# A hybrid decoder block on one core: the indexer's preparation taken off GpSimd, its key before the latents, the latents behind two more gate tiles

## The chip, the cores and the metric

One NeuronCore of a Trainium2 chip runs the whole kernel. The metric is device time in microseconds of one execution. Engines are named as in the profile: PE (TensorE matmul), PEld (its weight loads), DVE (VectorE), ACT (ScalarE), POOL (GpSimd) and SP (SyncE, which only issues transfers).

## The reference, cut to what matters

The block takes x (1024 tokens, 1024 channels), normalises it and projects it with one wide weight. The projection feeds a sparse attention whose 256 keys per query are picked by an indexer, a latent attention, and two sigmoid gates that merge them; a gated MLP with a causal convolution follows.

```python
hn = rmsnorm(h, norm_mix_g[l])
proj = jnp.einsum('bsd,de->bse', hn, w_in[l])
(a_q, a_k, a_v, i_q, i_k, i_w, b_cq, b_ckv, b_kr, g_a, g_b) = jnp.split(proj, IN_OFFSETS, axis=-1)
i_q = apply_rope(i_q.reshape(b, s, IDX_HEADS, IDX_DIM), cos_i, sin_i, IDX_ROT_DIM) * (IDX_DIM ** -0.5)
i_k = apply_rope(rmsnorm(i_k, idx_k_norm_g[l])[:, :, None, :], cos_i, sin_i, IDX_ROT_DIM)[:, :, 0, :]
o_a = indexed_sparse_attention(a_q, a_k, a_v, i_q, i_k, i_w, positions, topk)
c_q, c_kv = rmsnorm(b_cq, q_a_norm_g[l]), rmsnorm(b_ckv, kv_a_norm_g[l])
o_b = latent_attention(q_nope, q_rope, k_nope, k_rope, v_b, positions)
merged = jax.nn.sigmoid(g_a) * y_a + jax.nn.sigmoid(g_b) * y_b
```

Inside the sparse attention, for each block of 128 queries:

```python
dots = jnp.einsum('bqhd,bsd->bqhs', qib, ki)
iscore = jnp.einsum('bqh,bqhs->bqs', wib, jax.nn.relu(dots))
_, idx = lax.top_k(jnp.where(causal, iscore, -jnp.inf), topk)
```

## The kernel before, in words

**Products.** Every float32 operand is split into a high part (a copy into the fp32r type) and a low part (source minus high part). `mm3` (lines 176 to 189; the matmuls are L179, L180, L181) makes a product of three matmuls: high by high, high by low, low by high. `split` (L146) makes the parts: by default the high part is a copy on ACT (L149), the low part a subtraction on POOL (L155, which runs on DVE where a caller asks for it). `wload` (L521) fetches a piece of a weight through SP into one of three ring tiles (L496) and splits it.

**Stages around the change.** `load_x` loads and splits x and the weights `w_c2`. `chunk_kv` (L596) projects all eight blocks of 128 tokens with `w_c2` to 488 columns: the indexer's key (columns 0 to 63), its head weights (64 to 71), the query latent (72 to 327), the key latent (328 to 455) and the rotary key (456 to 487). ACT evacuates each block (L608) and takes sums of squares (L611). DVE then scales all three normalised parts (L627), applies the key's gain (L629), rotates the key and the rotary key (`rope`, L195 to L199), and SP stores the latents' rows to DRAM (L635, eight transfers). POOL writes the key twice, side by side (L638), so that a transpose on PE (L642) gives it on both halves of the partitions; ACT and DVE make its high and low parts (L643, L644).

`chunk_iq` (L671) projects the indexer's queries of blocks 2 to 7 with `w_c1`. `query` evacuates a block on ACT (L682) and rotates it on DVE; `stack` doubles its heads on POOL (`twice`, L660), transposes on PE (L651) and makes the parts on ACT and DVE (L653, L654). `indexer` (L729) then forms, head by head, scores on PE (L723), their relu on ACT (L742) and the weighted sum on DVE (L747). `chunk_a` (L966) projects the attention's queries and keys/values with `w_c3` and `w_c4` (four and two pieces of 128 x 1024) and stores them to DRAM through POOL's queue (L981). After that come the gate projections (`gates`, L985: eight weight tiles of `w_g` up to EARLY, then two up to NEXT; a tile is two halves of 512 tokens, each 24 matmuls; DVE takes each half out of PSUM, L1002). Beside them DVE searches the threshold of the top 256 (`guess`, L760; its counting step is L798).

`latents` (L1012) loads the stored rows again (L1021, six buffers), transposes them on PE (L1023) into three of the four single-bank PSUM tiles, and splits them (L1031, L1032). More gate tiles follow (10 to 13), then the latent attention. `prep_a` and `attn_a` (L1265, L1303) load the stored keys and queries for the sparse attention (L1274, L1297, L1314) and double them on POOL (L1275, L660) before the transposes.

**What sets the order.** The program text gives a priority; when the kernel is built, a planner simulates the engines and fixes one order of instructions for each engine. On the chip each engine and each issuing queue goes through its order and waits at the first instruction that is not ready. Tiles share memory: a tile whose place was used by an earlier one waits until that one is no longer read. The raw tiles of `chunk_iq` lie where `chunk_kv` kept its rows, so they also wait for the transfers of L635.

Of the kernel before, what the change touches and what calls it, by code (L numbers as in the profile page):

```python
# [10 lines left out]
F32 = mybir.dt.float32  # L11
# [6 lines left out]
OP = mybir.AluOpType  # L18
# [7 lines left out]
NKV = 2  # L26
# [82 lines left out]
class Block:  # L109
# [126 lines left out]
    def run(self):  # L236
# [55 lines left out]
        if self.causal:  # L292
            self.gates(None, go, range(EARLY, NEXT))
        self.latents(lat)
# [3 lines left out]
        self.gates(wg, go, range(NEXT if self.causal else 0, MID))  # L298
# [235 lines left out]
    def load_x(self, rawx, tmp):  # L534
# [9 lines left out]
        for kt in range(8):  # L544
            if kt == 2:
                self.prologue()
                if not self.causal:
                    self.positions(tmp)
            if kt == 0:
                w += self.cweights("w_c2", [0], "dve")  # L550
            st = self.t(rawx, [P, 1024], F32, tag="raw", bufs=3)
            parts = [slice(0, 512), slice(512, 1024)] if kt == 0 else [slice(0, 1024)]
            for cs in parts:
                nc.sync.dma_start(st[:, cs], a["xT"][kt * P:(kt + 1) * P, cs])
            if kt % 2 == 0 and kt:
                w += self.cweights("w_c2", [kt // 2], "dve")
# [24 lines left out]
    def cweights(self, name, js=range(4), eng_hi="act"):  # L581
        return [self.wload(self.w1, name, j, 4, eng_hi) for j in js]
# [13 lines left out]
    def chunk_kv(self, rawx, w):  # L596
# [22 lines left out]
        v.tensor_tensor(rs, rs, r3, op=OP.mult)  # L619
        self.iw = self.t(c, [P, NB, NH])  # L620
        v.tensor_scalar(self.iw, braw[:, :, HD:HD + NH], NH ** -0.5, None, op0=OP.mult)
        v.tensor_tensor(self.iw, self.iw, self.r[:, :, None].to_broadcast([P, NB, NH]), op=OP.mult)
        x = braw[:, :, 456:488]
        v.tensor_tensor(x, x, self.r[:, :, None].to_broadcast([P, NB, 32]), op=OP.mult)
        for k, (o, n) in enumerate(segs):
            x = braw[:, :, o:o + n]
            v.tensor_tensor(x, x, rs[:, k, :, None].to_broadcast([P, NB, n]), op=OP.mult)  # L627
        x = braw[:, :, :HD]
        v.tensor_tensor(x, x, self.gik[:, None, :].to_broadcast([P, NB, HD]), op=OP.mult)  # L629
        rt = self.kd[:, 768:].rearrange("p (b t n) -> p b t n", b=NB, t=2)  # L630
        self.rope(braw[:, :, 0:16].rearrange("p b (t n) -> p b t n", t=2), self.cos[:, :, ::2],
                  self.sin2[:, :, :, ::2], rt[:, :, :, 0:8])
        self.rope(braw[:, :, 456:488].rearrange("p b (t n) -> p b t n", t=2), self.cos, self.sin2, rt)
        for b in range(NB):
            nc.sync.dma_start(self.lat_d[b], braw[:, b, 72:W2N])  # L635
        kd = self.t(rawx, [P, S], F32, tag="raw", bufs=3)
# [7 lines left out]
        v.tensor_tensor(self.ikll, ps, self.ikhh.bitcast(F32), op=OP.subtract)  # L644

# [11 lines left out]
    def twice(self, pool, x, nh, tag, bufs=2):  # L657

        y = self.t(pool, [P, nh * 2 * HD], F32, tag=tag, bufs=bufs)
        self.nc.gpsimd.tensor_scalar(y.rearrange("p (h t d) -> p h t d", h=nh, t=2),  # L660
                                     x.rearrange("p (h d) -> p h d", h=nh)[:, :, None, :].to_broadcast([P, nh, 2, HD]),
                                     1.0, 0.0, op0=OP.mult, op1=OP.add)
        return y
# [7 lines left out]
    def chunk_iq(self, rp):  # L671
# [3 lines left out]
        w = self.cweights("w_c1")  # L675
# [11 lines left out]
        def stack(b):  # L687
            q[b] = self.qstack(self.twice(rp, raw[b], NH, "rawi", 1), IDX_SC, (8192, 5120, 4096)[b % 3])
# [576 lines left out]
    def prep_a(self):  # L1265
# [6 lines left out]
        def one(b):  # L1272
            raw = self.t(self.ring, [P, S], F32, tag="st", bufs=3)
            nc.sync.dma_start(raw[:, :256], self.akv_d[b])  # L1274
            nc.gpsimd.tensor_scalar(raw[:, 256:512].rearrange("p (h t d) -> p h t d", h=NKV, t=2),  # L1275
                                    raw[:, :P].rearrange("p (h d) -> p h d", h=NKV)[:, :, None, :]
                                    .to_broadcast([P, NKV, 2, HD]), 1.0, 0.0, op0=OP.mult, op1=OP.add)
# [17 lines left out]
        def first(n):  # L1295
            raw = self.t(self.ring, [P, S], F32, tag="st", bufs=3)[:, :512]
            nc.sync.dma_start(raw, self.aq_d[ORDER_A[n]])  # L1297
            self.qa.append(self.qstack(self.twice(self.ring, raw, NH, "st", 3), -SC_A, 7168 + 1024 * n))
# [4 lines left out]
    def attn_a(self, sp, ap, before, rest):  # L1303
# [738 lines left out]
```

## Time and profile before

| | us |
|---|---|
| three timed runs | 1594.61, 1597.29, 1597.31 |
| median | 1597.29 |
| the profiled execution, time | 1594.33 |
| the profiled execution, span of its instructions | 1592.5 |
| busy: PE, DVE, POOL, ACT | 1507.2, 1187.3, 910.5, 789.4 |

The span runs from the first to the last instruction; the time adds 1.8 us around it. A busy time is the union of the engine's instructions. "Idle before" an instruction is the gap on its own engine, put down to the work whose end released it.

### The profile page before, as it was taken

The page shows a single profiled execution, that of the slowest core. Times are in us where ns is not written, and L with a number is a line of the kernel's source. Part 1 is how long each engine was busy: PE and PEld are TensorE (multiplying, and loading weights), DVE is VectorE, ACT ScalarE, POOL GpSimd, SP SyncE. Part 2 cuts the span into 40 slices and gives each one's busy share as a digit, 9 for nine tenths or more (in the row PEclk, how much of TensorE's full clock was granted, in tenths as well). Part 3 has the DMA queues.
Part 4 walks back from the last instruction along what each step waited for, and adds up shares of the span by engine and source line. Part 5 has one row for each costly group of instructions (what it writes and reads, how often), then busy time and mean ns, then how long its engine had stood idle before and what let it go on. Part 6 is the DMA issues. An engine that isn't in the chain of part 4 may idle for free.

```text
span 1592.5 us, 21976 instructions
## 1 busy us (share of the span) xinstructions
PE 1507.2 (95%) x7586; PEld 1255.6 (79%) x7586; DVE 1187.3 (75%) x1860; ACT 789.4 (50%) x1454; POOL 910.5 (57%) x769
## 2 busy tenths in 40 slices
PE   9989999989899999999999989999999999989996
PEld 7768888867688877998878877888888887767874
DVE  7368999934588888885636668777777766896996
ACT  4545522223377788775434444444444444434445
POOL 4142122411667767654732399777777772487684
PEclk9989999999999999999999999999999999999999
DMA  7331133330300022213762132222222204964343
GB/s 256 108 105 46 54 105 97 111 115 27 106 14 17 14 83 93 76 56 118 238 198 87 53 93 80 80 80 82 81 84 84 85 36 162 329 210 127 126 137 123
DMA packets 74842, 166.25 MB, mean 104 GB/s; under 512 B 9634, under 2 KB 14114, under 8 KB 74722
## 3 DMA queue, kind: packets, MB, share of 16 engines
q1 hardware_dynamic: 62640, 139.59, 26.6%
q10 hardware_dynamic: 9490, 16.79, 2.8%
q0 software_dynamic: 2592, 8.39, 1.4%
q8 instruction: 61, 1.00, 0.3%
q14 instruction: 59, 0.48, 0.1%
HBM read 123.94 MB, written 40.53 MB: 103 GB/s over the span
## 4 chain that ended last, share of the span: by engine, by line
PE 66%; DVE 18%; issue 5%; ACT 4%; POOL 3%; DMA 3%; SPq 0%; ACTq 0%; DVEq 0%; POOLq 0%
PE tc L179 17%; PE tc L180 17%; PE tc L181 17%; PE tc L723 6%; DVE tc L155 3%; DVE tc L798 2%; DMA tc<-tc 2%; PE tc L1375 2%; PE tc L1228 2%; PE tc L1360 2%; PE tc L1209 1%; DVE tc L1136 1%; DVE tc L1002 1%; DVE tc L1159 1%; PE tc L651 1%
## 5 line engine op out<-in xcount | busy, mean ns | idle before, releaser
L179 PE MATMUL tc<-tc,tc 128*128 128x512 f32 (+2 forms) x1464 | 542.7, 374 | 9.7 <-ACT tc L1561 2.7
L181 PE MATMUL tc<-tc,tc 128*128 128x512 f32 (+2 forms) x1464 | 544.1, 372 | 4.3 <-DVE tc L155 4.3
L180 PE MATMUL tc<-tc,tc 128*128 128x512 f32 (+2 forms) x1464 | 544.3, 372 | 1.4 <-POOL tc L155 1.4
L155 POOL TENSOR_TENSOR tc<-tc,tc 128x512 fp32r<-128x512 f32 (+2 forms) x182 | 301.0, 1660 | 267.0 <-ACT tc L149 253.7
L149 ACT ACTIVATE tc<-tc 128x512 fp32r<-128x512 f32 (+1 forms) x362 | 230.5, 659 | 352.4 <-PE tc L180 242.1
L179 PEld LDWEIGHTS tc<-tc,tc 128*128 128x128 f32 x1464 | 277.3, 190 | 61.5 <-ACT tc L1561 3.0
L181 PEld LDWEIGHTS tc<-tc,tc 128*128 128x128 f32 x1464 | 277.3, 189 | 54.6 <-DVE tc L155 4.8
L180 PEld LDWEIGHTS tc<-tc,tc 128*128 128x128 f32 x1464 | 277.7, 190 | 50.5 <-POOL tc L155 2.1
L155 DVE TENSOR_TENSOR tc<-tc,tc 128x512 fp32r<-128x512 f32 x184 | 224.4, 1253 | 46.2 <-ACT tc L149 46.0
L180 PE MATMUL tc<-tc 128*128 128x512 f32 (+1 forms) x380 | 149.4, 395 | 11.6 <-DVE tc L155 11.3
L181 PE MATMUL tc<-tc 128*128 128x512 f32 (+1 forms) x380 | 146.7, 389 | 0.5 <-DVE tc L155 0.5
L179 PE MATMUL tc<-tc 128*128 128x512 f32 (+1 forms) x380 | 140.2, 389 | 1.5 <-ACT tc L149 1.2
L1169 POOL TENSOR_SCALAR tc<-tc,tc 128x128 f32<-128x128 f32 (+7 forms) x128 | 95.1, 748 | 62.2 <-DVE tc L1168 50.7
L1167 ACT ACTIVATE tc<-tc,tc 128x128 f32<-128x128 f32 (+7 forms) x128 | 96.3, 753 | 31.8 <-DVE tc L1161 13.6
L1744 DVE SCALAR_TENSOR_TENSOR tc<-tc,tc,tc 128x1023 f32<-128x1023 f32 x44 | 65.6, 1493 | 51.3 <-ACT tc L1743 51.2
L723 PE MATMUL tc<-tc 128*128 128x384 f32 (+4 forms) x352 | 89.8, 366 | 10.2 <-DVE tc L654 6.6
L180 PEld LDWEIGHTS tc<-tc 128*128 128x128 f32 x380 | 71.6, 188 | 34.8 <-DVE tc L155 20.2
L1745 DVE SCALAR_TENSOR_TENSOR tc<-tc,tc,tc 128x1022 f32<-128x1022 f32 x44 | 94.3, 2144 | 1.4
L179 PEld LDWEIGHTS tc<-tc 128*128 128x128 f32 x380 | 71.6, 189 | 17.3 <-ACT tc L149 2.2
L181 PEld LDWEIGHTS tc<-tc 128*128 128x128 f32 x380 | 71.8, 189 | 15.5 <-DVE tc L155 1.7
L723 PE MATMUL tc<-tc,tc 128*128 128x512 f32 (+4 forms) x288 | 75.2, 360 | 9.1 <-ACT tc L1167 8.2
L723 PEld LDWEIGHTS tc<-tc 128*128 128x128 f32 x352 | 60.6, 191 | 19.9 <-DVE tc L654 7.5
(266 smaller groups left out, 2429.8 us busy)
## 6 DMA issues: line engine op xcount, KB each, us to landing
tc<-tc SPq DMA_DIRECT2D x144, 256.0 KB, 3.7
tc<-in_w_up SPq DMA_DIRECT2D x44, 512.0 KB, 4.1
tc<-in_w_down SPq DMA_DIRECT2D x77, 256.0 KB, 3.7
tc<-tc ACTq DMA_DIRECT2D x52, 256.0 KB, 2.0
tc<-tc SPq DMA_DIRECT2D x20, 512.0 KB, 2.6
tc<-in_w_g SPq DMA_DIRECT2D x16, 512.0 KB, 3.6
tc<-tc POOLq DMA_DIRECT2D x24, 256.0 KB, 2.4
tc<-in_w_c SPq DMA_DIRECT2D x10, 512.0 KB, 4.4
```

The source lines that it names most:

```text
L149: self.last_split = nc.scalar.activation(hi, src, AF.Copy)
L155: e.tensor_tensor(lo, src, hi.bitcast(F32), op=OP.subtract)
L179: x = [mm(ps, lhs[0], rhs[0], start=start, stop=False, **kw), mm(ps, lhs[0], rhs[1], start=False, stop=False, **kw), mm(ps, lhs[1], rhs[0] ...
L180: mm(ps, lhs[0], rhs[1], start=False, stop=False, **kw),
L181: mm(ps, lhs[1], rhs[0], start=False, stop=stop, **kw)]
L723: self.last_score = mm(ps[:, j * 512:j * 512 + n], l, r[:, o:o + n], start=i == 0, stop=i == len(lhs) - 1)
L798: v.tensor_scalar(x, self.isc[b], c[:, j:j + 1], 0.0, op0=OP.is_ge, op1=OP.add, accum_out=cnt[:, j:j + 1])
L1167: self.last_exp = nc.scalar.activation(p3, src, AF.Exp, bias=nm, scale=-1.0, accum_out=l)
L1169: nc.gpsimd.tensor_scalar(p, p, l, 0.0, op0=OP.mult, op1=OP.add)
L1228: self.last_value = mm(po[0][:, 512 - y.shape[-1]:], lhs, y, start=kt == 0 and i == 0, stop=kt == last and i == 1, skip_group_check=True)
L1744: v.scalar_tensor_tensor(o[:, 1:], x[:, :S - 1], cw[:, t, 1:2], o[:, 1:], op0=OP.mult, op1=OP.add)
L1745: v.scalar_tensor_tensor(o[:, 2:], x[:, :S - 2], cw[:, t, 0:1], o[:, 2:], op0=OP.mult, op1=OP.add)
```

## The change

- `chunk_kv` prepares the indexer's key alone first (scaling by its own factor, gain, rotation), doubles it with one copy on ACT, and returns the rest (latents, rotary key, the eight stores) as a function that is called after the loading of `w_c1` has been written.
- The low parts of `w_c3` and `w_c4` are made on DVE; those of `w_c2` and `w_c1` stay on POOL.
- The indexer's queries are doubled by a copy on ACT.
- The attention's keys and queries are doubled by the load itself: `twice` issues two transfers on SP, each writing every other 64 columns. The tile of the undoubled rows goes; the doubled one has two buffers instead of one.
- Gate tiles 10 and 11 are written before `latents` instead of behind it.

```diff
-        self.chunk_kv(rawx, w)
+        latent_rows = self.chunk_kv(rawx, w)
+        w = self.cweights("w_c1", eng_lo="pool")
+        latent_rows()
...
-        self.chunk_iq(raw)
+        self.chunk_iq(raw, w)
...
+        first = NEXT + 2 if self.causal else 0
+        if self.causal:
+            self.gates(wg, go, range(NEXT, first))
         self.latents(lat)
...
-        self.gates(wg, go, range(NEXT if self.causal else 0, MID))
+        self.gates(wg, go, range(first, MID))
...
-    def cweights(self, name, js=range(4), eng_hi="act"):
-        return [self.wload(self.w1, name, j, 4, eng_hi) for j in js]
+    def cweights(self, name, js=range(4), eng_hi="act", eng_lo="dve"):
+        return [self.wload(self.w1, name, j, 4, eng_hi, eng_lo) for j in js]
...
+        x = braw[:, :, :HD]
+        v.tensor_tensor(x, x, rs[:, 0, :, None].to_broadcast([P, NB, HD]), op=OP.mult)
...
         kd = self.t(rawx, [P, S], F32, tag="raw", bufs=3)
-        for k in range(2):
-            nc.gpsimd.tensor_scalar(kd.rearrange("p (b t d) -> p b t d", b=NB, t=2)[:, :, k], braw[:, :, :HD], 1.0, 0.0,
-                                    op0=OP.mult, op1=OP.add)
+        nc.scalar.activation(kd.rearrange("p (b t d) -> p b t d", b=NB, t=2),
+                             braw[:, :, None, :HD].to_broadcast([P, NB, 2, HD]), AF.Copy)
...
+        def rest():
...
+            for k, (o, n) in list(enumerate(segs))[1:]:
+                x = braw[:, :, o:o + n]
+                v.tensor_tensor(x, x, rs[:, k, :, None].to_broadcast([P, NB, n]), op=OP.mult)
+            self.rope(braw[:, :, 456:488].rearrange("p b (t n) -> p b t n", t=2), self.cos, self.sin2, rt)
+            for b in range(NB):
+                nc.sync.dma_start(self.lat_d[b], braw[:, b, 72:W2N])
+        return rest
...
-    def twice(self, pool, x, nh, tag, bufs=2):
...
+    def twice(self, x, src, nh):
+
+        x = x[:, :nh * 2 * HD].rearrange("p (h t d) -> p h t d", h=nh, t=2)
+        for t in range(2):
+            self.nc.sync.dma_start(x[:, :, t], src.rearrange("p (h d) -> p h d", h=nh))
...
         def stack(b):
-            q[b] = self.qstack(self.twice(rp, raw[b], NH, "rawi", 1), IDX_SC, (8192, 5120, 4096)[b % 3])
+            y = self.t(rp, [P, S], F32, tag="rawi", bufs=1)
+            nc.scalar.activation(y.rearrange("p (h t d) -> p h t d", h=NH, t=2),
+                                 raw[b].rearrange("p (h d) -> p h d", h=NH)[:, :, None, :].to_broadcast([P, NH, 2, HD]),
+                                 AF.Copy)
+            q[b] = self.qstack(y, IDX_SC, (8192, 5120, 4096)[b % 3])
...
-            nc.sync.dma_start(raw[:, :256], self.akv_d[b])
...
+            nc.sync.dma_start(raw[:, P:256], self.akv_d[b][:, P:])
+            self.twice(raw[:, 256:], self.akv_d[b][:, :P], NKV)
...
-                one = self.t(at, [P, 512], F32, tag="qraw", bufs=2)
-                nc.sync.dma_start(one, self.aq_d[b])
-                raw = self.twice(at, one, NH, "qdup", QDUP)
+                raw = self.t(at, [P, S], F32, tag="qdup", bufs=2)
+                self.twice(raw, self.aq_d[b], NH)
```

## Rows read from the trace of the kernel before

**Rows 1.** The page, busy time, share of the span and instructions of each engine.

```profile
PE 1507.2 (95%) x7586; PEld 1255.6 (79%) x7586; DVE 1187.3 (75%) x1860; ACT 789.4 (50%) x1454; POOL 910.5 (57%) x769
```

**Rows 2.** What PE waited for from 0 to 300 us: total, times, longest.

```profile
PE tc L723 <- DVE tc L654: 6.6, 1, 6.6
PE tc L642 <- POOL tc L638: 2.1, 1, 2.1
...
PE tc L180 <- POOL tc L155: 1.4, 2, 0.7
```

**Rows 3.** Stretches: length, busy PE, PEld, DVE, ACT, POOL; granted clock, DMA share, GB/s.

```profile
76.00:80.00 4.00, 2.62 (x16) 2.30 (x17) 2.51 (x6) 1.49 (x2) 1.32 (x2) 1.00 0.26 98
101.00:107.00 6.00, 5.86 (x16) 5.19 (x17) 2.33 (x5) 1.96 (x4) 0.00 (x0) 0.50 0.18 71
200.00:320.00 120.00, 119.65 (x572) 100.52 (x570) 117.86 (x266) 29.36 (x40) 40.85 (x25) 1.00 0.33 106
324.00:327.00 3.00, 1.73 (x7) 1.44 (x8) 2.29 (x6) 1.45 (x3) 0.00 (x0) 0.50 0.47 175
```

**Rows 4.** Instructions in order of time, 85 to 102 us: start, duration, engine, line.

```profile
84.51 2.42 ACT L682 ACTIVATE tc<-tc,tc 128x512 f32<-128x512 f32 x4 [4.40 <-DMA tc<-tc]
...
87.96 8.13 POOL L155 TENSOR_TENSOR tc<-tc,tc 128x1024 fp32r<-128x1024 f32 x3 [0.85 <-ACT tc L149]
...
88.34 0.20 DVE L195 TENSOR_TENSOR tc<-tc,tc 128x64 f32<-128x64 f32 x1
...
89.19 2.35 DVE L199 TENSOR_TENSOR tc<-tc,tc 128x128 f32<-128x128 f32 x1
...
90.58 1.02 ACT L653 ACTIVATE tc<-tc 128x1024 fp32r<-128x1024 f32 x1 [0.19 <-PE tc L651]
...
99.86 1.23 DVE L654 SCALAR_TENSOR_TENSOR tc<-tc,tc 64x1024 fp32r<-64x1024 f32 x1
...
101.14 1.33 PE L723 MATMUL tc<-tc 128*128 128x384 f32 x3 [6.57 <-DVE tc L654]
```

**Rows 5.** DVE in order of time, 40 to 125 us: the key's chain.

```profile
70.29 4.03 DVE L627 TENSOR_TENSOR tc<-tc,tc 128x512 f32<-128x512 f32 x3
...
79.58 1.22 DVE L644 TENSOR_TENSOR tc<-tc,tc 128x1024 fp32r<-128x1024 f32 x1 [1.45 <-ACT tc L643]
```

**Rows 6.** PE in order of time, 318 to 331.5 us: the latents' transposes.

```profile
319.38 0.27 PE L1023 MATMUL tc<-tc,tc 128*128 128x128 f32 x1
324.09 0.48 PE L1023 MATMUL tc<-tc,tc 128*128 128x128 f32 x1 [4.44 <-DVE tc L1002]
325.75 2.82 PE L1023 MATMUL tc<-tc,tc 128*128 128x128 f32 x12 [1.18 <-DVE tc L1002]
329.16 0.33 PE L1023 MATMUL tc<-tc,tc 128*128 128x128 f32 x1 [0.59 <-DMA tc<-tc]
330.27 1.20 PE L1023 MATMUL tc<-tc,tc 128*128 128x128 f32 x9 [0.78 <-DMA tc<-tc]
```

**Rows 7.** DVE in order of time, 300 to 360 us: the evacuations of gate halves.

```profile
323.35 0.68 DVE L1002 TENSOR_TENSOR tc<-tc,tc 128x512 f32<-128x512 f32 x1
...
325.01 1.28 DVE L1002 TENSOR_TENSOR tc<-tc,tc 128x512 f32<-128x512 f32 x2
...
342.45 0.69 DVE L1002 TENSOR_TENSOR tc<-tc,tc 128x512 f32<-128x512 f32 x1 [4.75 <-PE tc L181]
```

**Rows 8.** All engines in order of time, 599.9 to 601.2 us: one block's queries.

```profile
599.96 1.03 POOL L660 TENSOR_SCALAR tc<-tc 128x1024 f32<-128x1024 f32 x1
...
601.05 0.33 PE L651 MATMUL tc<-tc,tc 128*128 128x128 f32 x1 [1.22 <-POOL tc L660]
```

**Rows 9.** SP's queue in order of time, 580 to 612 us: those queries' load.

```profile
584.26 0.43 SPq L1314 DMA_DIRECT2D tc<-tc  x1
```

**Rows 10.** Line L1314, loads of 256 KB in 2-KB runs.

```profile
DMA to landing us min/median/max: 2.5/3.0/3.5
```

**Rows 11.** Line L1274, loads of 128 KB in 1-KB runs.

```profile
DMA to landing us min/median/max: 2.0/2.0/3.6
```

More of the change, by code (lines that the diff above doesn't have):

```diff
@@ L549, in load_x @@
             if kt == 0:
-                w += self.cweights("w_c2", [0], "dve")
+                w += self.cweights("w_c2", [0], "dve", "pool")
             st = self.t(rawx, [P, 1024], F32, tag="raw", bufs=3)
@@ L555, in load_x @@
             if kt % 2 == 0 and kt:
-                w += self.cweights("w_c2", [kt // 2], "dve")
+                w += self.cweights("w_c2", [kt // 2], "dve", "pool")
             for cs in parts:
@@ L619, in chunk_kv @@
         v.tensor_tensor(rs, rs, r3, op=OP.mult)
+        rt = self.kd[:, 768:].rearrange("p (b t n) -> p b t n", b=NB, t=2)
+        x = braw[:, :, :HD]
+        v.tensor_tensor(x, x, rs[:, 0, :, None].to_broadcast([P, NB, HD]), op=OP.mult)
+        v.tensor_tensor(x, x, self.gik[:, None, :].to_broadcast([P, NB, HD]), op=OP.mult)
+        self.rope(braw[:, :, 0:16].rearrange("p b (t n) -> p b t n", t=2), self.cos[:, :, ::2],
+                  self.sin2[:, :, :, ::2], rt[:, :, :, 0:8])
+        kd = self.t(rawx, [P, S], F32, tag="raw", bufs=3)
+        nc.scalar.activation(kd.rearrange("p (b t d) -> p b t d", b=NB, t=2),
+                             braw[:, :, None, :HD].to_broadcast([P, NB, 2, HD]), AF.Copy)
         self.iw = self.t(c, [P, NB, NH])
@@ L622, in chunk_kv @@
         v.tensor_tensor(self.iw, self.iw, self.r[:, :, None].to_broadcast([P, NB, NH]), op=OP.mult)
[L623 to L636, printed above, removed]
-        for k in range(2):
-            nc.gpsimd.tensor_scalar(kd.rearrange("p (b t d) -> p b t d", b=NB, t=2)[:, :, k], braw[:, :, :HD], 1.0, 0.0,
-                                    op0=OP.mult, op1=OP.add)
         ps = self.psS()
@@ L644, in chunk_kv @@
         v.tensor_tensor(self.ikll, ps, self.ikhh.bitcast(F32), op=OP.subtract)
+        def rest():
+            x = braw[:, :, 456:488]
+            v.tensor_tensor(x, x, self.r[:, :, None].to_broadcast([P, NB, 32]), op=OP.mult)
+            for k, (o, n) in list(enumerate(segs))[1:]:
[5 more added lines that the diff above has]
+        return rest
     def qstack(self, raw, scale, off):
@@ L655, in qstack @@
         return q
-    def twice(self, pool, x, nh, tag, bufs=2):
[L659 to L663, printed above, removed]
+    def twice(self, x, src, nh):
+        x = x[:, :nh * 2 * HD].rearrange("p (h t d) -> p h t d", h=nh, t=2)
+        for t in range(2):
+            self.nc.sync.dma_start(x[:, :, t], src.rearrange("p (h d) -> p h d", h=nh))
     def rope8(self, pool, raw, nh, b):
@@ L669, in rope8, with chunk_iq @@
                   self.sin2[:, b, None, :, ::2].to_broadcast([P, nh, 2, 8]), rt[:, :nh])
-    def chunk_iq(self, rp):
+    def chunk_iq(self, rp, w):
         nc = self.nc
         blocks = range(2, NB) if self.causal else range(NB)
-        w = self.cweights("w_c1")
         self.rl = [self.kd, self.t(rp, [P, S])]
@@ L1295, in first @@
         def first(n):
-            raw = self.t(self.ring, [P, S], F32, tag="st", bufs=3)[:, :512]
-            nc.sync.dma_start(raw, self.aq_d[ORDER_A[n]])
-            self.qa.append(self.qstack(self.twice(self.ring, raw, NH, "st", 3), -SC_A, 7168 + 1024 * n))
+            raw = self.t(self.ring, [P, S], F32, tag="st", bufs=3)
+            self.twice(raw, self.aq_d[ORDER_A[n]], NH)
+            self.qa.append(self.qstack(raw, -SC_A, 7168 + 1024 * n))
         self.qa = []
```

3 lines of the change are left out of this document (removed).

## Prediction

> **What bounds the kernel now.** I read the page's busy times first: PE is busy for 95% of the span [rows 1], so time can come only from PE's gaps and from matmuls at the lower clock; POOL and DVE matter where PE waits for them. The view of PE's waits over the first 300 us then names three that this change touches [rows 2]: 6.6 us before the indexer's first scores (L723, for DVE's L654), 2.1 before the key's transposes (L642, for POOL's doubling), and two of together 1.4 before products with `w_c3` (L180, for low parts on POOL). The order of time around the longest shows why DVE was late. Until 88.5 us a step of the queries' rotation takes 0.20 us; at 87.96 POOL begins three low parts that last 8.13 us together, and now the same kind of step takes 2.35, about as long as one POOL instruction [rows 4]. L653 had ended at 91.6, yet L654 starts at 99.86, behind the rotations. The view of stretches shows the second price: a granted clock of 0.50 (the 1.2 GHz level) from 101 to 107 us with PE busy for 5.86 us, half of it, 2.9, lost; around the wait of 2.1 us the clock stayed at 1.00 [rows 3].
>
> The other place is at 324 us. PE in order of time shows the latents' transposes waiting 4.44, 1.18, 0.59 and 0.78 us, 7.0 in all, the first two for DVE's evacuation of gate halves [rows 6]. A half takes PE 5.44 us (the gap plus the evacuation of a stretch without backlog, 4.75 + 0.69 [rows 7]). The gates end at 319.4, so their last three halves ended at 308.5, 314.0 and 319.4; DVE took these out at 323.35 and from 325.01 on [rows 7], the first 14.8 us late. The latents need three of four PSUM tiles at once, a gate half one.
>
> **First scores, -8.8 us.** Removed: the four POOL subtractions of `w_c3`, with the hold on DVE. Between 89.19 and 99.86 DVE ran the last step of one rotation and the five of another, 1.2 us at 0.20 each; so 10.67 - 1.2, some 9.4 us, are freed. Added on DVE: four low parts at 1.22 us, by the nearest row of that shape, L644 [rows 5]. POOL ran three of them one behind the other from 87.96; the planner need not put all of these ahead of L654, and I take two, 2.4 us. L654 also comes later with the latents' stores: ACT's evacuations of the queries (and the rotations behind them) waited 4.40 us for these transfers [rows 4], and they are now issued behind the key's low part at the worst, 1.2 us later. So L654 ends near 101.1 - 9.4 + 2.4 + 1.2 = 95.3, and PE arrives at 101.14 - 6.57 - 1.4 = 93.2: a wait of 2.1 instead of 6.57 + 1.4. The other wait of 2.1 kept the clock, so the 2.9 come back too: 7.97 - 2.1 + 2.9 = 8.8. Ends: 10.9 if nothing is left, 0 if the planner puts all low parts and the later transfers in front and something else holds L654.
>
> **Key first, 0.** Of L627's 4.03 us for 3584 columns, 3072 leave the key's chain, 3.45 us [rows 5]; two POOL copies become one on ACT, some 1.02 by L653 [rows 4]. But PE's order was fixed by a plan, and the plan sees the shorter chain too: it will put L642 in front of some queries' products that now stand ahead of it, so that the wait of 2.1 need not shrink. Ends: -2.1, and +2.1 if it doubles. What is late next are the latents' rows, counted above.
>
> **Doublings on ACT, +1.0.** Six copies of about 1.02 us replace six on POOL of about the same length (1.03, L660 [rows 8]), so the chain to the transposes keeps its length. But ACT's order also carries the relus for which PE's scores wait. The cover is PE's other work: `w_c3`'s products are woven between. Ends: 0, and 5.1 if each of the last five holds a relu; I take one.
>
> **The two low parts of `w_c4`, 0.** 2.4 us on DVE behind 170 us, where DVE is as good as full: 117.86 of 120 us from 200 to 320 [rows 3]. PE hardly waits there because a gate half may be evacuated up to three halves (16.3 us) late. Ends: 0, and +2.4.
>
> **Latents behind two more tiles, -5.6.** Four halves, 21.8 us of PE work, now lie between the point where DVE's backlog is worst and the transposes. DVE's `guess` ended with the evacuations at 325; with the freed DVE time it ends earlier, while the transposes start about 22 us later in PE's order. So 4.44 and 1.18 go. The two waits for transfers stay: the last two loads need buffers that the first transposes free, and without the pause of 1.18 these waits grow by as much. The clock, 0.50 there [rows 3], is granted again: twelve transposes took 2.82, the last nine 1.20, at which rate twelve take 1.6, so 1.2 is lost [rows 6]. Sum: 5.62 - 1.2 + 1.2 = 5.6. Ends: -8.2 and 0. The cover between latents and latent attention shrinks to two gate tiles (21.8 us), enough for some 4 us of splitting.
>
> **Attention, -1.2.** Each block's queries lose a POOL copy of 1.03 us, and PE's one wait of 1.22 for it goes [rows 8]. SP gains an issue for each of eight query blocks and two for each of eight key blocks: 24 times some 0.43 us [rows 9], spread over all blocks; what stands behind them are mask, gate and weight loads with a block's time to spare. The load must land before L651: 601.05 - 584.26 = 16.8 us after the issue [rows 8, 9], against 2.5 to 3.5 to landing for 256 KB in runs of 2 KB [rows 10] and 2.0 for 128 KB in runs of 1 KB [rows 11]. Two loads in runs of 256 bytes are in no row. Bounds: if bytes count, 2 x 3.5 = 7 us, hidden; if each run costs what a 2-KB run costs, the 0.5 to 1.5 us above the 2.0 become 4 to 12 for 1024 runs, and the pair 10 to 26. I take the value near the rows on bytes. Ends: -2.4 (a second block's copy on POOL) and, as a case of its own, below.
>
> The Trainium skill speaks against this edit: "DMA: Bandwidth & Descriptors", section Specifications, asks for at least 512 bytes per piece for full rate and says that smaller ones are read, modified and written. By that rule alone, taken as half the rate, a pair would need an estimated 12 us, which the lead still covers, and the sum stays; the case in which it does not is the third rival. No row here shows pieces of 256 bytes in a load.
>
> **Sum.** -8.8 + 0 + 1.0 + 0 - 5.6 - 1.2 = -14.6 us against the profiled execution, with the 1.8 us around its span unchanged: 1594.33 - 14.6 = 1579.7. That execution lies 2.96 below the median of the runs, 1597.29, at their lower edge; on the median the sum gives 1582.7. I forecast **1581**, between them. What a measurement can tell from no change is about 0.2%, 3.2 us.
>
> **Rivals.** *Nothing left to wait for:* all gaps and both clock losses go, and the second POOL copy: 10.9 + 2.1 + 8.2 + 2.4 = 23.6, 1571. For it: from 101 to 107 us DVE is busy for 2.33 of 6 us [rows 3], so there is room to catch up; against it: PE's fixed order. Chance 0.12. *The first scores stay late:* low parts, later transfers and doublings fill DVE's and ACT's orders ahead of L654, the wait stays above 4 us (the clock fell at 4.44), and that term gives some 3 instead of 8.8: 1587. Chance 0.19.
>
> *Short runs set the time of a load (slower):* the pair takes 26 us instead of fitting into 16.8. Then each of the six later blocks comes up to 9 us late until the two buffers give a longer lead; three blocks at 9 are 27, less 13.4 for the other terms: about +14, 1610. With 10 us for a pair nothing happens; it decides from 16.8 us. For it: the count of runs is eightfold; against: lower bound 10 us. Chance 0.06.
>
> *DVE becomes the bound:* 7.3 us of low parts in a stretch in which it is full. If the freed 9 us are lost in waiting for PE's scores, the lag of 14.8 passes 16.3 and PE waits some 6 us at the last halves with the clock falling: the first term is given back and up to 6 lost, the latents' stays: 1592 to 1599. Against it: POOL's hold on DVE goes with each moved part. Chance 0.07. That the plan only moves the waits to other places is the last case, 1593 to 1601, with 0.06.
>
> **How the numbers follow.** The forecast's own cases, 1575 to 1587, have 0.50. The range of 1571 to 1592 holds these, the late scores and most of the best case, some 0.8. Faster by over 0.2% are the forecast and the first two rivals, with a little of the last two: 0.82. Of the rest of these two most lies within 0.2%, 0.08; beyond it are the short runs and some of both, 0.10.
>
> **What would show it.** Right: no DVE step of 2.3 us between 85 and 100; L654 by 96; PE's wait before L723 below 3 us and 1.00 as clock behind it; no wait of L1023 for L1002; L651 in the attention with no wait for a transfer. Wrong: a wait at L642 over 3 us, waits of L651 for DMA, or gate products waiting for L1002 before the latents.

## The result, and the profile after

The changed kernel takes 1580.03 us (median of four runs, 1577.30 to 1580.95) against 1595.95 for the kernel before on the same chip: a ratio of 0.9897, interval 0.9882 to 0.9913. It is 15.9 us faster, within the range and 1 us below the forecast. Where kernels below are compared with each other, the difference of their ratios is taken, times 1596 us. Its profiled execution took 1577.30 us, 17.0 below that of the kernel before. Line numbers below are the changed kernel's own: the scores are L734, the key's transposes L640, the indexer's and the attention's query transposes L661, their low part L664, the latents' transposes L1034, the evacuation of gate halves L1013.

The page of the changed kernel, busy times, answers to [rows 1]; what PE waited for from 0 to 300 us answers to [rows 2].

```profile
PE 1504.7 (96%) x7586; PEld 1256.5 (80%) x7586; DVE 1175.8 (75%) x1866; ACT 795.7 (51%) x1461; POOL 872.7 (55%) x739
```

```profile
PE tc L734 <- DVE tc L664: 3.5, 5, 1.4
PE tc L640 <- ACT tc L633: 1.8, 1, 1.8
```

The one wait of 6.6 us is gone, five of at most 1.4 have come (in a second profile of the same kernel, e12 below, five of at most 2.1, 4.6 in all); POOL's low parts stand in no wait any more; the key's transposes wait nearly as long as before. POOL has lost 38 us of work. The order of time, 84 to 108 us, against [rows 4]:

```profile
88.43 2.56 DVE L155 TENSOR_TENSOR tc<-tc,tc 128x1024 fp32r<-128x1024 f32 x2 [0.39 <-ACT tc L149]
91.17 1.23 DVE L155 TENSOR_TENSOR tc<-tc,tc 128x1024 fp32r<-128x1024 f32 x1 [0.17 <-ACT tc L149]
92.28 1.03 ACT L663 ACTIVATE tc<-tc 128x1024 fp32r<-128x1024 f32 x1 [0.18 <-PE tc L661]
92.31 0.22 DVE L195 TENSOR_TENSOR tc<-tc,tc 128x64 f32<-128x64 f32 x1
93.34 1.23 DVE L664 SCALAR_TENSOR_TENSOR tc<-tc,tc 64x1024 fp32r<-64x1024 f32 x1 [0.68 <-ACT tc L663]
94.63 0.97 PE L734 MATMUL tc<-tc 128*128 128x384 f32 x4 [0.27 <-DVE tc L664]
```

DVE makes three low parts in front of L664 (2.56 and 1.23 us), its rotation steps take 0.22 us, L664 ends at 94.57, and PE has waited 0.27 us. Stretches of the changed kernel (length, busy PE, PEld, DVE, ACT, POOL, granted clock, DMA share, GB/s), against [rows 3]:

```profile
78.00:80.00 2.00, 2.00 (x9) 1.80 (x8) 0.00 (x0) 0.83 (x1) 0.00 (x0) 0.50 0.73 270
80.00:82.00 2.00, 2.00 (x7) 1.57 (x7) 1.22 (x1) 0.78 (x2) 0.00 (x0) 0.68 1.03 372
95.00:100.00 5.00, 5.00 (x25) 4.26 (x24) 3.64 (x6) 2.06 (x5) 0.00 (x0) 1.00 0.59 190
330.00:340.00 10.00, 8.39 (x49) 6.97 (x48) 4.83 (x7) 5.29 (x9) 2.88 (x3) 1.00 0.47 166
```

The clock is 1.00 (2.4 GHz) behind the first scores and around the latents, 0.50 (1.2 GHz) just behind the key's wait; PE is busy all through those 4 us, so some 1.6 us (2 x 0.50 + 2 x 0.32) are lost there. PE in order of time at the latents' transposes, against [rows 6]:

```profile
332.88 1.69 PE L1034 MATMUL tc<-tc,tc 128*128 128x128 f32 x14
335.99 0.33 PE L1034 MATMUL tc<-tc,tc 128*128 128x128 f32 x1 [1.43 <-DMA tc<-tc]
336.51 1.20 PE L1034 MATMUL tc<-tc,tc 128*128 128x128 f32 x9 [0.19 <-DMA tc<-tc]
```

Both waits for DVE's evacuations are gone; only the last two loads are late, by 1.6 us in all. So much for the gains. In the attention, the wait of L661 for POOL's copy has gone too, and yet that stretch got longer. From the first to the last of the attention's matmuls (L1368, L1383) the changed kernel needs 156.0 us, the kernel before 154.1. What PE waited for in that stretch, and two parts of it (length, busy PE, granted clock, DMA share, GB/s):

```profile
PE tc L734 <- DVE tc L1176: 1.5, 5, 0.4
PE tc L734 <- ACT tc L1178: 1.4, 3, 0.7
PE tc L1383 <- ACT tc L1371: 1.3, 3, 0.8
PE tc L1368 <- DVE tc L1372: 0.8, 3, 0.3
PE tc L1368 <- POOL tc L1180: 0.8, 1, 0.8
PE tc L734 <- DVE tc L664: 0.7, 1, 0.7
PE tc L1383 <- DVE tc L1372: 0.2, 1, 0.2
```

```profile
584.00:592.00 8.00, 5.84 (x35) 0.87 0.51 133
592.00:600.00 8.00, 8.00 (x48) 0.92 0.00 1
```

These waits sum to 6.7 us, and in both parts the mean granted clock is below 1.00. No transfer is among them. (The kernel with the two moves alone, below, is the counterpart.) But one wait for a transfer stands 10 us ahead of that stretch, at the transposes of a block's queries; the second line is SP's issue of the pair of loads that they read:

```profile
565.88 1.06 PE L661 MATMUL tc<-tc,tc 128*128 128x128 f32 x8 [1.49 <-DMA tc<-tc]
560.33 1.23 SPq L671 DMA_DIRECT2D tc<-tc  x2
```

PE was ready at 564.39, 4 us after the issue. This pair goes through the ring's tiles, and before it SP had waited 3.1 us for the transposes of the attention's keys (L1292) to free one.

### The profile page after: what moved, and what is told of

Same layout as the page of the kernel before. It is cut to its first block, busy times and chain, and to the rows that moved or that the text cites. A ratio compares the mean times of both kernels' runs of the same rounds, so it can differ in the third digit from the quotient of the medians.

```text
span 1575.5 us, 22027 instructions
## 1 busy us (share of the span) xinstructions
PE 1504.7 (96%) x7586; PEld 1256.5 (80%) x7586; DVE 1175.8 (75%) x1866; ACT 795.7 (51%) x1461; POOL 872.7 (55%) x739
## 4 chain that ended last, share of the span: by engine, by line
PE 68%; DVE 12%; ACT 5%; issue 5%; DMA 5%; POOL 4%; SPq 0%; ACTq 0%; DVEq 0%; POOLq 0%
PE tc L180 18%; PE tc L179 18%; PE tc L181 18%; PE tc L734 6%; DVE tc L155 3%; DMA tc<-tc 3%; PE tc L1383 2%; PE tc L1239 2%; PE tc L1368 1%; PE tc L1220 1%; POOL tc L155 1%; DVE tc L1147 1%; ACT tc L1178 1%; ACT tc L149 1%; DVE tc L1170 1%
## 5 line engine op out<-in xcount | busy, mean ns | idle before, releaser
L155 POOL TENSOR_TENSOR tc<-tc,tc 128x512 fp32r<-128x512 f32 (+2 forms) x176 | 282.7, 1611 | 305.4 <-ACT tc L149 287.6
L155 DVE TENSOR_TENSOR tc<-tc,tc 128x512 fp32r<-128x512 f32 (+1 forms) x190 | 229.4, 1240 | 47.8 <-ACT tc L149 47.5
L1180 POOL TENSOR_SCALAR tc<-tc,tc 128x128 f32<-128x128 f32 (+7 forms) x128 | 95.4, 751 | 68.6 <-DVE tc L1179 54.9
L734 PE MATMUL tc<-tc 128*128 128x384 f32 (+4 forms) x352 | 89.1, 363 | 7.9 <-DVE tc L664 4.3
L734 PE MATMUL tc<-tc,tc 128*128 128x512 f32 (+4 forms) x288 | 75.0, 360 | 8.0 <-ACT tc L1178 7.1
L734 PEld LDWEIGHTS tc<-tc 128*128 128x128 f32 x352 | 60.3, 190 | 18.6 <-DVE tc L664 6.7
```

The costliest lines, as they stand in the source:

```text
L155: e.tensor_tensor(lo, src, hi.bitcast(F32), op=OP.subtract)
L734: self.last_score = mm(ps[:, j * 512:j * 512 + n], l, r[:, o:o + n], start=i == 0, stop=i == len(lhs) - 1)
L1180: nc.gpsimd.tensor_scalar(p, p, l, 0.0, op0=OP.mult, op1=OP.add)
```

## Where the time went, stage by stage

Six landmarks cut each trace: PE's first transpose of the key, of the row scales behind the indexer, of `prep_v`, the attention's first and last matmul (the two lines named above), and PE's last matmul. Each column is the difference of two start times in us; the last one runs to the end of PE's last matmul. The indexer stands in the second, the latents in the third, the attention's transfers in the fourth and fifth.

| kernel | to key | key to row scales | to `prep_v` | to attention | attention | rest |
|---|---|---|---|---|---|---|
| before | 77.4 | 131.4 | 171.5 | 210.1 | 154.1 | 835.2 |
| changed | 77.5 | 123.0 | 164.3 | 210.8 | 156.0 | 832.1 |
| changed, again (e12) | 74.3 | 124.3 | 164.2 | 212.8 | 156.8 | 830.8 |
| e1 low parts on POOL | 75.2 | 127.2 | 164.7 | 214.3 | 157.6 | 832.3 |
| e2 latents before the tiles | 75.4 | 122.5 | 174.2 | 210.9 | 156.5 | 833.4 |
| e3 attention doubled on POOL | 78.5 | 124.3 | 164.2 | 209.7 | 154.1 | 834.0 |
| e4 key not first | 78.2 | 122.6 | 164.2 | 210.6 | 156.1 | 831.9 |
| e8 key held first | 78.5 | 125.1 | 164.2 | 211.9 | 156.3 | 832.3 |
| e9 queries on POOL | 78.8 | 123.1 | 164.3 | 211.5 | 156.3 | 832.6 |
| e10 shorter runs | 76.2 | 122.8 | 164.1 | 212.2 | 155.6 | 831.2 |
| e5 before + low parts | 78.7 | 123.4 | 172.1 | 210.9 | 154.1 | 832.0 |
| e6 before + tiles | 78.8 | 130.1 | 164.4 | 211.8 | 154.2 | 834.4 |
| e7 before + both | 79.1 | 121.7 | 164.3 | 209.8 | 154.1 | 830.7 |
| e11 as e7, eight buffers | 78.1 | 121.6 | 222.1 | 209.8 | 154.3 | 834.2 |

The second and third rows of numbers are one kernel profiled twice: they differ by 3.2 us before the key, 2.0 ahead of the attention, 1.3 in the rest, and by at most 1.3 in the other columns. What an edit does is read in its own column; differences of that size elsewhere are put down to no edit.

## The experiments

### Parts of the change undone

**e1, the low parts back on POOL.**

```diff
-    def cweights(self, name, js=range(4), eng_hi="act", eng_lo="dve"):
+    def cweights(self, name, js=range(4), eng_hi="act", eng_lo="pool"):
```

> The changed kernel with the low parts of w_c3 and w_c4 back on POOL, all else as changed. Theory (POOL's subtractions hold up DVE instructions with two SBUF operands, and this made the first scores late): DVE steps of 2.3 us between 85 and 100 us come back, the first L664 ends after 99 us, PE waits 5 to 7 us before its first scores and goes on at 1.2 GHz; some 8 us over the changed kernel, 1588 us. Rival (the doublings on ACT and the key's place did it; POOL's low parts are only beside the path): first scores before 97 us, 1579 to 1582 us.

Measured: 1586.84 us, ratio 0.9950 (0.9932 to 0.9968), 8.5 us slower than the changed kernel. The order of time of this run shows the hold again:

```profile
86.24 7.08 POOL L155 TENSOR_TENSOR tc<-tc,tc 128x1024 fp32r<-128x1024 f32 x3 [27.15 <-ACT tc L149]
89.90 1.18 DVE L195 TENSOR_TENSOR tc<-tc,tc 128x64 f32<-128x64 f32 x1 [4.10 <-ACT tc L689]
91.00 2.40 DVE L196 TENSOR_TENSOR tc<-tc,tc 128x64 f32<-128x64 f32 x1
93.32 0.35 DVE L198 TENSOR_TENSOR tc<-tc,tc 128x64 f32<-128x64 f32 x2
93.79 2.42 POOL L155 TENSOR_TENSOR tc<-tc,tc 128x1024 fp32r<-128x1024 f32 x1 [0.47 <-ACT tc L149]
94.03 1.23 DVE L664 SCALAR_TENSOR_TENSOR tc<-tc,tc 64x1024 fp32r<-64x1024 f32 x1
95.31 1.16 PE L734 MATMUL tc<-tc 128*128 128x384 f32 x4 [3.67 <-DVE tc L664]
```

While POOL runs its two-input subtractions, a DVE step of 0.22 us takes 1.18 and 2.40; when POOL's three have ended (93.32), two steps take 0.35 together. That is the step on which the first term rests, switched off and on by one word. The Trainium skill, "GPSIMD Engine Reference", in its table of specifications, has POOL share its memory interfaces with VectorE, in contention with VectorE instructions that have two inputs in SBUF; the trace agrees, with these numbers. Not every step is held: L664, which takes one of its two inputs from PSUM, ran beside POOL's fourth subtraction in the 1.23 us that it needs without one. Only two steps were held here, not five, so the wait came to 3.67 us, less than the 5 to 7 expected and the 6.57 of before: how many steps meet POOL is the plan's doing. By its own column the edit costs 4.2 us (127.2 against 123.0), half of the 8.5. Another 3.5 lie ahead of the attention, where the clock is at 0.50 from 448 to 450 and from 489 to 491 us, while the changed kernel shows 1.00 from 440 to 500; no run ties that to the low parts.

**e2, the two tiles behind the latents again.**

```diff
-        first = NEXT + 2 if self.causal else 0
-        if self.causal:
-            self.gates(wg, go, range(NEXT, first))
...
-        self.gates(wg, go, range(first, MID))
+        self.gates(wg, go, range(NEXT if self.causal else 0, MID))
```

> The changed kernel with gate tiles 10 and 11 behind the latents again, all else as changed. Theory (the two tiles cover DVE's backlog at the end of the gates): the transposes of the latents wait 4 to 6 us for L1002 again and the clock falls there; 1586 us. Rival (the moved low parts already took the backlog away, so the two tiles bring nothing by themselves): waits for L1002 below 1.5 us, 1579 to 1582 us.

Measured: 1590.78 us, ratio 0.9977 (0.9962 to 0.9992): 12.8 us slower, twice what was expected. PE's waits from 300 to 345 us in this run:

```profile
PE tc L1031 <- DVE tc L1010: 8.2, 2, 5.6
PE tc L1031 <- DMA tc<-tc: 1.4, 2, 0.8
```

The waits for DVE's evacuations are 8.2 us, where the kernel before had 5.62 [rows 6]; the column up to `prep_v` is 9.9 above the changed kernel's. The waits grow as PE reaches the row scales earlier: at 208.8 us in the kernel before 5.62, at 202.1 in e5 6.2, at 197.9 here 8.2. So PE seems to come to the latents further ahead of DVE, which fits these three and was not tried by itself. The profiled execution, 1586.59 us at a clock of 0.989, is the fastest of ten; the others have 0.982 to 0.986, so the clock has a part in the 12.8 too.

**e3, the attention's rows doubled on POOL again** (both `twice` and the keys' load as before; the first lines):

```diff
-    def twice(self, x, src, nh):
+    def twice(self, pool, x, nh, tag, bufs=2):
...
-            self.twice(raw, self.aq_d[ORDER_A[n]], NH)
+            nc.sync.dma_start(raw, self.aq_d[ORDER_A[n]])
```

> The changed kernel with the attention's keys and queries loaded once and doubled on POOL as before, all else as changed. Theory (doubling by transfers costs time: from the latent attention's first transposes to the last of the sparse attention the changed kernel is 2.6 us slower than the one before): 2 to 3 us faster than the changed kernel, 1577.5 us, without PE's wait of 1.5 us for a transfer. Rival (as forecast, POOL's copies cost PE 1.2 us, and the loss comes from elsewhere): 1580 to 1582 us, with a wait of L661 for POOL.

Measured: 1578.80 us, ratio 0.9899 (0.9871 to 0.9928); by time it can't be told from the changed kernel, and neither theory is decided by it. The attention's own column decides: 154.1 us, as before, although PE waits for POOL's copy again:

```profile
PE tc L661 <- POOL tc L670: 1.2, 1, 1.2
```

The wait of 1.49 us for a load, which the changed kernel has ahead of this stretch, is gone.

**e4, the key prepared together with the latents** (still doubled on ACT):

```diff
-        latent_rows = self.chunk_kv(rawx, w)
+        self.chunk_kv(rawx, w)
...
-        latent_rows()
...
```

> The changed kernel with the key prepared with the latents as before (its doubling stays on ACT), all else as changed. Theory (the planner runs the latents' scaling on DVE before the key's gain in both, so the key's place in the text gains nothing): key's transposes at 77 to 78 us, 1579 to 1582 us. Rival (the place is worth what leaves the chain, up to 3 us): transposes after 80 us, 1583 us.

Measured: 1579.22 us, ratio 0.9902 (0.9874 to 0.9930). Writing the key first gains nothing: the column behind the key's transposes is 122.6 against 123.0. (The transposes themselves wait 0.3 us here, less than in the changed kernel, but PE had already waited 2.9 us at 54 us for an evacuation on ACT, L612.) The changed kernel's order of time says why:

```profile
70.72 0.69 DVE L628 TENSOR_TENSOR tc<-tc,tc 128x512 f32<-128x512 f32 x1
71.33 3.42 DVE L650 TENSOR_TENSOR tc<-tc,tc 128x2048 f32<-128x2048 f32 x2
74.67 0.68 DVE L629 TENSOR_TENSOR tc<-tc,tc 128x512 f32<-128x512 f32 x1
```

Between the key's scaling (L628) and its gain (L629) the planner put 3.42 us of the latents' scaling (L650). First in the program is not first on the engine.

**e8, the key held first**, by a dependency that keeps L650 behind its rotation:

```diff
...
+            with self.tc.issue_after(key.ins):
+                for k, (o, n) in list(enumerate(segs))[1:]:
+                    x = braw[:, :, o:o + n]
+                    v.tensor_tensor(x, x, rs[:, k, :, None].to_broadcast([P, NB, n]), op=OP.mult)
```

> The changed kernel, where the latents' scaling is made to wait on DVE until the key is rotated. Theory (PE's order follows the plan, which sees the shorter chain too): the key's transposes run some 3 us earlier but PE still waits 1.5 us or more for them, and the stores of the latents' rows go out 2 us or more later; 1579 to 1582 us, no gain. Rival (the key's chain sets the wait): PE's wait before the key's transposes below 0.5 us; 1577 to 1578 us.

Measured: 1580.30 us, ratio 0.9889 (0.9865 to 0.9913). The key's transposes wait for nothing now, which was the rival's side (here too PE had waited 2.9 us at 54 us), and still nothing is gained: the column up to the row scales is 125.1. The scores' waits in PE's list, 0 to 300 us, are 0.8 us more than e12's 4.6:

```profile
PE tc L736 <- DVE tc L666: 5.4, 5, 2.1
```

**e9, the indexer's queries doubled on POOL again.**

```diff
-            nc.scalar.activation(y.rearrange("p (h t d) -> p h t d", h=NH, t=2),
+            nc.gpsimd.tensor_scalar(y.rearrange("p (h t d) -> p h t d", h=NH, t=2),
...
```

> The changed kernel with one part undone: the indexer queries' heads are doubled on POOL again, the key's row still by ScalarE. The changed kernel took 1580.0 us, and a kernel with only the low parts on VectorE and the two gate tiles moved took 1574.1; so the doublings and the key's order together cost some 6 us. Theory: ScalarE is not the place where it goes; its doubling of about 1 us per block lies beside the matmuls, and most of the loss is in the attention's transfers and in where the planner puts the weights' work: 1579 to 1581, as the changed kernel, with TensorE's wait of its first scores between 0 and 2 us. Rival: ScalarE's doublings push its clamps of the scores and delay the scores of the next block (TensorE waits of 1.36, 0.52 and 1.09 us for L664 in the changed kernel): then these waits shrink, the stretch from the key's transposes to the first of the row scales loses some 3 us of its 123, and the time is 1576 to 1577.

Measured: 1580.04 us, ratio 0.9904 (0.9889 to 0.9920), column 123.1. The theory stands: ACT's doublings cost nothing that can be measured. The rival's waits for L664 did go, but one for POOL's copy came in their place; PE's list of this run:

```profile
PE tc L661 <- POOL tc L696: 2.8, 1, 2.8
```

### What a load in short runs costs

**e10, runs of 128 bytes instead of 256, twice as many transfers.**

```diff
+        src = src.rearrange("p (h d) -> p h d", h=nh)
...
-            self.nc.sync.dma_start(x[:, :, t], src.rearrange("p (h d) -> p h d", h=nh))
+            for o in (0, 32):
+                self.nc.sync.dma_start(x[:, :, t, o:o + 32], src[:, :, o:o + 32])
```

> The changed kernel with each transfer that doubles the attention's queries or keys cut into two, each of half the columns of every head: runs of 128 bytes instead of 256, the bytes in all the same, twice as many transfers. In the changed kernel the loads of 256 KB land 3.6 to 4.8 us after their issue, where the kernel before's loads of the same bytes in runs of 2 KB took 2.5 to 3.5. Theory: the time to landing goes with the number of runs, and there are as many of these per transfer as before (1024 of half the size), with two transfers in flight for each one: the later of two lands 6 to 8 us after its issue, TensorE waits for the queries' transposes in most blocks, and the kernel takes 1584 to 1592. Rival: it goes with the bytes: each transfer of 128 KB lands in 2.5 to 3.5 us and the kernel stays at 1578 to 1582.

Measured: 1577.5 us, a single run, so the time decides nothing. The loading line serves keys (64 KB in 256 runs a load) and queries (256 KB in 1024 runs); the queries' loads alone, those after 555 us, first in the changed kernel, then in this one, where each is 128 KB in 1024 runs:

```profile
DMA to landing us min/median/max: 3.6/4.1/4.8
```

```profile
DMA to landing us min/median/max: 2.5/3.7/4.3
```

Neither was quite right. Half the bytes in as many runs land 0.4 us sooner at the median, so bytes set little of it; but several transfers in flight do not add up either, and the later of two comes nowhere near 6 to 8 us. PE waits 2.2 us in all for these loads, in two waits ahead of the attention's stretch, against 1.49 in the changed kernel.

### The parts alone, on the kernel before

**e5, the low parts on DVE alone.**

```diff
...
-                w.extend(self.cweights(name, range(4 if nh == NH else 2)))
+                w.extend(self.cweights(name, range(4 if nh == NH else 2), "act", "dve"))
```

> The kernel before with one edit: the low parts of w_c3 and w_c4 on DVE (doublings stay on POOL, latents where they were). Theory (two stages in a row: what PE wins at the first scores it loses at the latents, because it only runs further ahead of DVE there): first scores 4 to 7 us earlier, but the waits for L1002 at the latents grow from 5.6 to 8 us or more; 2 to 5 us faster than before. Rival (the terms add as in the prediction): 8 to 9 us faster, waits at the latents as before.

Measured: 1586.95 us, ratio 0.9941 (0.9921 to 0.9962), 9.4 faster. The indexer's column gains 8.0; the latents' column stays (172.1). PE's waits, 0 to 300 and 300 to 345 us:

```profile
PE tc L651 <- POOL tc L660: 3.8, 1, 3.8
...
PE tc L723 <- DVE tc L654: 0.3, 1, 0.3
```

```profile
PE tc L1023 <- DVE tc L1002: 6.2, 2, 3.5
```

The wait of 6.6 for L654 is 0.3, one of 3.8 for POOL's doubling stands ahead of it, and the latents wait 6.2 for DVE instead of the 8 or more that I expected. The rival, terms that add, came nearer.

**e6, the two tiles ahead of the latents alone** (on the kernel before).

```diff
+        first = NEXT + 2 if self.causal else 0
+        if self.causal:
+            self.gates(wg, go, range(NEXT, first))
         self.latents(lat)
...
```

> The kernel before with one edit: gate tiles 10 and 11 ahead of the latents. Theory: waits of the latents for L1002 gone, those for transfers about as they were, first scores as before; 5 to 8 us faster. Rival (PE meets DVE's backlog in the gate tiles instead): waits of gate products for L1002, less than 3 us faster.

Measured: 1588.05 us, ratio 0.9954 (0.9934 to 0.9975), 7.3 faster, as expected. The latents' column goes from 171.5 to 164.4; the first scores wait 6.6 us as before; the one wait left at the latents is for a load:

```profile
PE tc L1026 <- DMA tc<-tc: 1.2, 1, 1.2
```

**e7, both edits, of e5 and e6**, and nothing else of the change.

> The kernel before with both edits: low parts of w_c3 and w_c4 on DVE, gate tiles 10 and 11 ahead of the latents. Theory (the two need each other): more than the sum of the two alone, 11 to 15 us faster, nearly the whole change. Rival (the doublings on ACT or by transfers carry a good part): 7 to 10 us faster.

Measured: **1574.08 us**, ratio 0.9855 (0.9836 to 0.9875): more than expected, and faster than both kernels. The columns are as good as a sum: 121.7 from the one move, 164.3 from the other, the attention as before (154.1). The same two stretches of the attention:

```profile
583.00:591.00 8.00, 5.41 (x35) 1.00 0.35 100
591.00:599.00 8.00, 7.75 (x48) 1.00 0.22 60
```

PE's waits between the attention's first and last matmul sum here to 5.9 us, POOL's copy among them, and the clock stays at 1.00; in the changed kernel they sum to 6.7 without that copy, with 0.87 and 0.92.

**e11, both, and eight buffers for the latents' rows instead of six**, to take away the wait for the last two loads.

```diff
...
-                raw = self.t(bx, [P, 416], F32, tag="lat", bufs=6)
+                raw = self.t(bx, [P, 416], F32, tag="lat", bufs=8)
```

> The kernel before with two moves alone (the low parts of w_c3 and w_c4 on VectorE, two gate tiles ahead of the latents' transposes; 1574.1 us when it was measured) and with eight buffers for the latents' blocks instead of six, so that no block's load waits for a buffer. Theory: the waits of about 1.6 us for the last two blocks' loads at the latents' transposes go, and nothing else changes: 1572 to 1573.5. Rival: the loads are late because of their queue and not because of the buffers, or other work fills the time: 1574 to 1575. Either way it is faster than the changed kernel by 5 to 8 us on the same chip.

Measured: 1636.09 us, ratio 1.0267 (1.0251 to 1.0283), 66 us slower than without the two buffers. PE's waits from 330 to 420 us, the line that begins a threshold search, and two stretches (all engines, as above):

```profile
PE tc L866 <- DVE tc L862: 56.9, 1, 56.9
PE tc L1026 <- DVE tc L1035: 1.2, 1, 1.2
```

```profile
337.02 1.34 DVE L783 BATCH_NORM_STATS2 tc<-tc 128x6 f32<-128x320 f32 x3
```

```profile
280.00:300.00 20.00, 20.00 (x94) 16.65 (x93) 2.36 (x4) 7.42 (x10) 10.97 (x6) 1.00 0.38 120
380.00:400.00 20.00, 0.00 (x0) 0.00 (x0) 19.41 (x37) 0.00 (x0) 0.00 (x0) 0.50 0.00 0
```

The waits for loads are gone, as expected. But DVE's last threshold search, which in e7 began by 203.0 us, begins at 337, right behind the latents' last transpose (336.2); from 280 to 300 us DVE is nearly idle, and then PE waits 56.9 us for the search's flag. By the code the search's memory is taken after the latents' has been given back; that the larger pool now shares its place with the search's is the likely reason, argued from this order and not tried by itself.

**e12, the changed kernel again**, on e11's chip.

> The changed kernel itself, unaltered, beside the one with two moves alone, on the same chip. Theory: as before, 1579 to 1581, ratio to the kernel before 0.989 to 0.991, and 5 to 8 us slower than the two moves alone. Rival: the difference of 6 us between the two was one of chips or runs: then it stands at 1574 to 1577 here, or the other at 1578 to 1580.

Measured: 1579.09 us, ratio 0.9900 (0.9885 to 0.9916), as the theory said. So the distance between it and the two moves alone, 7 us by the ratios, is not one chip's.

## Why the prediction was right, point by point

The two moves that I had named carry the result, and with nearly the sizes that I gave them; one term had the wrong sign.

**First scores, key and doublings, -7.8 together; measured -8.4** (131.4 to 123.0; e12 -7.1). The mechanism is the one argued: e1 brings two of the held steps back and gives up 4.2, e5 takes them all away by itself and gains 8.0. Within it, two of my guesses cancelled. I allowed a wait of 2.1 us at the first scores; it was 0.27, with L664 0.7 us earlier than I had worked out. Against that stand later waits that I had not counted, the other four of the five in PE's list (3.2 us), and the clock behind the key's wait: I had put nothing for it, because the kernel before kept 1.00 there, and it took some 1.6. *Key first, 0*, is the right size by e4 and e8, but not for the reason given. I expected the plan to move the key's transposes forward in PE's order; in both kernels PE executes 300 matmuls before the first of them. The plan left DVE's chain as long as it was, with the latents' scaling inside it (e4), and where the chain is made shorter nothing is gained either (e8). *Doublings on ACT, +1.0*: e9 shows no cost, but 1.0 is less than one kernel's two profiles differ.

**The low parts of `w_c4`, 0.** Not isolated. In e5 they are there with the old order, and the latents' column is 0.6 us longer than before, less than one kernel's two profiles differ: no price is seen.

**Latents, -5.6; measured -7.2** (171.5 to 164.3), alone -7.1 in e6. The step that failed: without the pause, the waits for the last two loads should have grown by 1.2; they went from 1.37 to 1.62. With 0.25 in its place the sum is 5.62 + 1.2 - 0.25 = 6.6. What I had missed altogether is that the term depends on the first. With the scores early and the old order of tiles, PE waits 8.2 us for evacuations (e2) and the column is 9.9 above the changed kernel's. In e5, the old order with early scores, it is 7.8 above e7's. So the tiles are worth 7.1 without the early scores (e6) and 7.8 to 9.9 with them. By time the two moves give 23 us in e7 against 9.4 + 7.3 alone; by the columns of indexer and latents together it is 16.9 against 15.8, so most of that surplus lies where no edit is.

**Attention, -1.2; measured +1.9 in the stretch.** This is the wrong step: "PE's one wait of 1.22 for it goes" was right, that the time goes with it was not. In all eight profiles with doubling by transfers (the changed kernel, e1, e2, e4, e8, e9, e10, e12) the column is 155.6 to 157.6; in the six with POOL's copy it is 154.1 to 154.3. The stretch, in the kernel before, the changed one and e10 (length, busy PE, granted clock, DMA share, GB/s):

```profile
590.40:744.50 154.10, 147.68 (x961) 1.00 0.24 77
575.60:731.60 156.00, 148.63 (x959) 0.99 0.29 84
575.30:730.90 155.60, 147.87 (x959) 1.00 0.33 85
```

Of the 1.9 us, 1.0 is PE busy for longer, at a clock below full, and 0.9 is PE idle. The clock is not the whole cause: e10 keeps 1.00 and is still 1.5 longer than the kernel before, nearly all of it idle. What POOL's wait leaves behind is a different order with other waits, 6.7 us instead of 5.9, among them one of 0.8 for another POOL instruction (L1180). Why the order brings these, and why the clock fell, is open.

The lead was wrong as well. The 16.8 us were read at one block and taken for all; the pair behind the wait of 1.49 us had 4, and a wait of these transposes for a transfer was my own sign of being wrong. The changed kernel, e1, e2, e4, e9 and e10 have 1.3 to 2.2 us of such waits ahead of the stretch; in e8 and e12 PE waits 1.2 and 1.3 at the same transposes, put down to DVE; the kernels with POOL's copy have no wait there.

**The sum.** By columns the change gave -8.4 - 7.2 + 0.7 + 1.9 = -13.0, where I had -14.6. Its profiled execution is 17.0 lower because the rest, which no edit touches, came out 3.1 shorter, and 1.0 more lies behind PE's last matmul. The kernel before and e6 have 835.2 and 834.4 there, e3 834.0 with most of the change in it: I put it down to no part of the change. That the forecast came within 1 us of the median is luck to that extent: two errors of 3 us, in the attention and in the rest, cancelled.

**The rivals.** *Short runs*: no load took longer than 4.8 us to land, at twice the count of runs 4.3, far from 16.8; my upper bound, in which each run costs what a 2-KB run costs, is refuted. What made one late was a lead of 4 us. The rule of the Trainium skill ("DMA: Bandwidth & Descriptors", Specifications) has the right direction: 4.1 at the median against 3.0 for 2-KB runs [rows 10], though with two loads in flight instead of one. The estimate by half the rate, 12 us for a pair, is more than twice what was measured: 4.8 at the most for a load, the second issued 0.6 behind the first. *Nothing left to wait for* came true at the first scores, not behind them. *The first scores stay late*, *DVE becomes the bound* and *the plan moves the waits* did not come; a little of the last one did, in the attention.

**What stays open.** The two moves alone are some 7 us faster than the whole change (0.9855 against 0.9900, intervals apart; 5.0 by the medians, 1574.08 against 1579.09). 1.9 of it is the attention; 1.3 and 1.0 lie in the columns of the indexer and ahead of the attention, no more than one kernel's two profiles differ, though the wait of 1.49 for a load stands in the latter. Some of the rest goes with the clock: over a whole run it is 0.990 on the mean of e7's four runs and 0.988 on that of the changed kernel's nine, which over 1575 us is an estimated 3 us (the attention's part included). Undoing the attention's transfers, the queries' doubling or the key's order one at a time gave none of it back in time. Undoing two of the three together was not tried.

## What to carry to other kernels

Where a DVE step suddenly takes ten times as long, look at what POOL is doing in the same microsecond: moving POOL's two-input work onto DVE can free more of DVE than it costs (here DVE's busy time fell from 1187.3 to 1175.8 us with six low parts of 1.2 more on it). When work is moved so that one stage starts earlier, price the next stage's queue again, for the engine behind may not have caught up. And taking away a visible wait of 1 us by a different route is worth nothing until the stage's whole length is shorter; measure landmarks on both sides of it. A lead read at one load is not the lead of the others: look at each issue of the line.

## What the runs showed that I had not expected

**The clock is not told by the length of the wait alone.** Around the key's wait of 2.1 us the kernel before kept 1.00 [rows 3]; behind a wait of 1.83 us the changed kernel shows 0.50 from 78 to 80 us. In the attention, 8 us with PE busy for 5.84 had 0.87 and were followed by 0.92; 8 us with 5.41 had 1.00 and were followed by 1.00. Nor does one kernel do the same twice: in e12 the key's wait of 1.2 us kept 1.00, and behind a wait of 2.1 at the scores the clock was 0.53 from 104 to 106 us.

**Two more buffers of 1.7 KB per partition cost 66 us** (e11): another engine's work, 57 us of it on PE's path, moved behind the stage that they were meant to help.

**Halving the bytes of a load hardly made it land sooner**: 4.1 us at the median with 1024 runs of 256 bytes, 3.7 with 1024 of 128 (e10).
